# PEER routing in fewer DVE steps, one ring of gather buffers for u and v, and 768 gathered columns of v

## The chip, the cores and the metric

The kernel runs on one core of a Trainium2 chip. The metric is the device time of one execution in microseconds, the median of three runs. PE is the matrix engine, DVE the vector engine, ACT the scalar engine, POOL is GpSimd, SP the queue from which plain loads and stores are issued.

## The reference, cut to what matters

Two blocks follow each other on 256 tokens of width 2048, all in f32: a block of two layers (sparse attention, retention) and a block with an attention mixer and a PEER layer. The change lies in the PEER layer alone, which picks for each token and each of 8 heads 16 of 16,384 experts by two half keys of 128, and adds up the picked rows of v, weighted by the gelu of the product with the picked rows of u:

```python
def block(hb):                                   # 128 tokens at a time, D = 2048
    q = (hb @ w_query).reshape(PEER_BLOCK, PEER_HEADS, 2, D_KEY // 2)
    s = jnp.einsum('thpc,hpnc->thpn', q, sub_keys)
    top_s, top_i = lax.top_k(s, PEER_TOPK)
    cand_s = (top_s[:, :, 0, :, None] + top_s[:, :, 1, None, :]).reshape(PEER_BLOCK, PEER_HEADS, -1)
    cand_i = (top_i[:, :, 0, :, None] * N_KEYS + top_i[:, :, 1, None, :]).reshape(PEER_BLOCK, PEER_HEADS, -1)
    best_s, best_j = lax.top_k(cand_s, PEER_TOPK)
    idx = jnp.take_along_axis(cand_i, best_j, axis=-1)
    g = jax.nn.softmax(best_s, axis=-1)
    u_sel = jnp.take(u, idx, axis=0)
    a = jax.nn.gelu(jnp.einsum('thkd,td->thk', u_sel, hb), approximate=False)
    v_sel = jnp.take(v, idx, axis=0)
    return jnp.einsum('thk,thkd->td', (g * a), v_sel)
```

## The kernel before

The two attention blocks fill the first 1,780 us; their instructions are the same before and after the change. The PEER layer that follows is written as operations handed to a planner (`Plan`). Each has an engine, a cost in us, a key, what it waits for and which buffers of which ring it takes and frees. `run` keeps a clock for each engine, takes the operation that can start first (among near equals the one with the lowest key) and emits it; the order in which each engine then executes is fixed. Transfers are modelled by one rate, 340 KB per us, and operations marked `two` on DVE and POOL exclude each other in the plan.

The stages of the PEER layer, by what they compute:

- **Queries and routing** (`plan_query`, `plan_route`): 16 units, one for each head and half of the tokens (t). In a unit, DVE takes the best 16 of each half key's 128 scores (L2026, L2027), adds them to 256 candidate sums (`cand`, L1553), takes the best 16 of those with their places `bj` (a row and a column of the 16 x 16 sums, L1563 and L1564), casts the places to bf16 (L1566), marks the place of each among 16 (`eq`, L1568), multiplies the marks with the half keys' indices `tif` (cast at L1551, multiplied at L1579), and sums along the last axis to two numbers each (`keyno`, L1581). The expert's row number is formed from the two (`idx`, L1584 and L1585). POOL negates the largest sum (`nm`, L1573, an operation of its own in the plan), and ACT takes the exponential for the softmax (L1576).
- **Gathers of u** (`plan_gather_u`): for each of the 256 pairs (head, rank, t) one indirect DMA from POOL's queue (L1684) fetches 128 rows of the first 1,024 columns of u, 512 KB. Its product with the tokens is either one DVE instruction (a dot, L1690; 167 of them) or a product on POOL (L1696, 89) with a sum on ACT (L1697). The planner chooses.
- **Scores** (`plan_scores`): the other 1,024 columns of u are loaded in full, 128 blocks of 128 experts, 512 KB each. They are transposed on PE, split into a high part (`uhi`, ACT, L1738) and a rest (`ulo`, DVE, L1742), and multiplied with the tokens (L1750 to L1752) into the table `S` of 128 x 128 x 256.
- **Picks** (`plan_digits`, `plan_keyno`, `plan_pick`, `plan_coef`): 64 groups of four tokens. One-hot rows come out of a product of digit codes (the far product, L1800, and a Relu on ACT, L1804), multiply `S` on PE (L1809), and a select on DVE (`pjunk`, L1815) takes the picked scores. The codes come from a constant `spread` that is loaded when the stage opens and multiplied out on DVE (`digits`, L1434).
- **Weights** (`plan_weights`): the picked experts' weights are written back over `S`, again with one-hot products (`ohb`, L1877; S copied by ACT, L1892).
- **v** (`plan_gather_v`, `plan_out`): for the first GV = 736 columns of v, 256 indirect gathers (L1925) are each scaled and added into `vacc` by DVE (L1932). The first 90 (EARLY) start when their buffers allow, the others are paced by the dense loads. The other 1,312 columns are loaded in full, 128 tiles of 128 experts (`vraw`, L1959); ACT makes `vhi` (L1963) and `wh`, DVE `vlo` (L1967) and `wl` (L1975), and PE runs 18 matmuls on each (L1980): three products, two halves of the tokens, pieces of 512, 512 and 288 columns.

Buffers around it: three slots for gathers of u in the early pool `ud`, and three more (`rg`) once routing is over. The early ones are given up when the scores near their end; the last gathers of u, and four buffers (`rx`) for gathers of v, go on side by side, and when the last dot is done the three of `rg` join the ring of v. The slots of `vraw` (four) lie in a pool that also holds the picks' and the weights' one-hot tiles and is opened anew (`open_out`) when the weights are done.

## Time and profile before

| | us |
|---|---|
| median of 3 runs | 3259.75 |
| lowest, highest | 3255.08, 3261.12 |
| the profiled execution | 3261.98 |
| its span, first to last instruction | 3260.3 |

Over the span PE is busy 2897.5 us (89%), DVE 2422.6 (74%), ACT 1550.9 (48%) and POOL 1113.1 (34%); the mean granted TensorE clock is 0.950 of full speed. A busy matrix engine over the whole span doesn't mean that it bounds each stage: the slices of the page show its share, the clock and the DMA rate rise and fall with the stages, and a stage is read by the engine or the queue that has no idle time in it. Durations below come from the profiled execution.

### The profile page before, as it was taken

How to read it: one execution, taken by the hardware profiler on the slowest of the kernel's cores; microseconds unless marked ns; L12 is line 12 of the kernel's file. 1: busy time of each engine (PE TensorE's matmuls, PEld its weight loads, DVE VectorE, ACT ScalarE, POOL GpSimd, SP SyncE). 2: the span in 40 equal slices, each digit the busy share in tenths (PEclk: the TensorE clock that was granted, in tenths of full speed). 3: DMA queues.
4: the chain of work that ended last, by engine and by line, in shares of the span. 5: the costliest groups of instructions: out<-in, count | busy, mean ns of one | idle time of the engine just before them, and what ended most of it. 6: DMA issues, size and time to landing. Idle time of an engine off the chain costs nothing.

```text
span 3260.3 us, 46369 instructions
## 1 busy us (share of the span) xinstructions
PE 2897.5 (89%) x16646; PEld 2461.6 (76%) x16646; DVE 2422.6 (74%) x4207; ACT 1550.9 (48%) x2529; POOL 1113.1 (34%) x805
## 2 busy tenths in 40 slices
PE   3598989789999999999998769798887799799998
PEld 1386667667788779888887768788886587688887
DVE  7969886867856654565555989778786789788886
ACT  5555554545444544454554435434343258344443
POOL 3324431412000000000000445557776657555541
PEclk9699999899999999999998989999998699899999
DMA  8777886766555554545456536799996558999997
GB/s 297 243 242 246 279 273 186 249 211 215 174 165 164 162 175 128 164 125 148 130 181 223 172 117 217 258 348 332 326 329 220 187 171 253 339 343 333 334 332 231
DMA packets 294611, 751.52 MB, mean 231 GB/s; under 512 B 33518, under 2 KB 40612, under 8 KB 293996
## 3 DMA queue, kind: packets, MB, share of 16 engines
q1 hardware_dynamic: 236432, 515.65, 49.9%
q0 software_dynamic: 57344, 230.72, 20.3%
q8 instruction: 131, 2.15, 0.3%
q10 hardware_dynamic: 604, 2.19, 0.2%
q14 instruction: 100, 0.82, 0.1%
HBM read 741.64 MB, written 6.82 MB: 230 GB/s over the span
## 4 chain that ended last, share of the span: by engine, by line
PE 53%; DVE 15%; DMA 12%; issue 6%; POOL 6%; ACT 3%; SPq 0%; DVEq 0%; POOLq 0%; ACTq 0%
PE b_mm L1980 11%; PE b_mm L393 7%; PE b_mm L394 7%; PE b_mm L392 7%; DMA mraw<-in_w_mod 6%; DMA gathered<-in_peer_u,idx 5%; PE b_at L1980 3%; DVE gathered L1690 2%; PE b_mm L414 2%; PE b_mm L412 2%; POOL gathered L1684 2%; PE b_mm L413 2%; DVE lo L367 2%; POOL gathered L1696 2%; PE b_at L1809 2%
## 5 line engine op out<-in xcount | busy, mean ns | idle before, releaser
L367 DVE TENSOR_TENSOR lo<-raw,hi 128x1024 fp32r<-128x1024 f32 (+2 forms) x456 | 573.7, 1260 | 351.7 <-ACT hi L366 349.8
L366 ACT CAST hi<-raw 128x1024 fp32r<-128x1024 f32 (+2 forms) x456 | 464.4, 1021 | 454.1 <-PE b_mm L394 285.1
L393 PE MATMUL b_mm<-lo,hh 128*128 128x512 f32 (+1 forms) x1536 | 620.6, 405 | 39.0 <-DVE lo L367 35.9
L394 PE MATMUL b_mm<-hi,hl 128*128 128x512 f32 (+1 forms) x1536 | 604.7, 398 | 0.3 <-DVE hl L644 0.3
L392 PE MATMUL b_mm<-hi,hh 128*128 128x512 f32 (+1 forms) x1536 | 580.7, 401 | 9.6 <-ACT hi L366 6.6
L1925 POOL DMA_INDIRECT gathered<-in_peer_v,idx x256 | 324.8, 1269 | 251.8 <-DVE vacc L1932 226.6
L1684 POOL DMA_INDIRECT gathered<-in_peer_u,idx x256 | 295.8, 1155 | 286.7 <-ACT gathered L1697 163.9
L393 PEld LDWEIGHTS b_mm<-lo,hh 128*128 128x128 f32 x1536 | 295.7, 192 | 118.5 <-DVE lo L367 59.6
L392 PEld LDWEIGHTS b_mm<-hi,hh 128*128 128x128 f32 x1536 | 292.6, 191 | 84.0 <-ACT hi L366 11.2
L394 PEld LDWEIGHTS b_mm<-hi,hl 128*128 128x128 f32 x1536 | 294.1, 192 | 63.0 <-DVE hl L644 1.7
L560 POOL TENSOR_TENSOR macc<-macc,mraw 128x512 f32<-128x512 f32 x112 | 183.9, 1642 | 419.1 <-ACT mraw L558 386.9
L1752 PE MATMUL b_mm<-hd,ulo 128*128 128x256 f32 x1024 | 301.3, 294 | 28.9 <-DVE ulo L1742 28.7
L1750 PE MATMUL b_mm<-hd,uhi 128*128 128x256 f32 x1024 | 309.4, 302 | 12.5 <-ACT uhi L1738 11.7
L1690 DVE SCALAR_TENSOR_TENSOR gathered<-gathered,hn 128x1024 f32<-128x1024 f32 x167 | 255.9, 1551 | 77.7 <-DMA gathered<-in_peer_u,idx 76.7
L1751 PE MATMUL b_mm<-hd,uhi 128*128 128x256 f32 x1024 | 295.5, 289 | 0.0
L1932 DVE SCALAR_TENSOR_TENSOR vacc<-gathered,cf,vacc 128x736 f32<-128x736 f32 x256 | 250.7, 979 | 9.4 <-DMA gathered<-in_peer_v,idx 8.4
L1752 PEld LDWEIGHTS b_mm<-hd,ulo 128*128 128x128 f32 x1024 | 201.7, 197 | 39.6 <-DVE ulo L1742 39.1
L1967 DVE TENSOR_TENSOR vlo<-vraw,vhi 128x1312 fp32r<-128x1312 f32 x128 | 195.1, 1524 | 46.6 <-ACT vhi L1963 46.6
L1696 POOL TENSOR_TENSOR gathered<-gathered,hn 128x1024 f32<-128x1024 f32 x89 | 213.6, 2400 | 20.4 <-DMA gathered<-in_peer_u,idx 18.9
L1963 ACT CAST vhi<-vraw 128x1312 fp32r<-128x1312 f32 x128 | 165.7, 1294 | 107.3 <-PE b_at L1980 99.3
L1750 PEld LDWEIGHTS b_mm<-hd,uhi 128*128 128x128 f32 x1024 | 202.3, 198 | 16.7 <-ACT uhi L1738 16.7
L1751 PEld LDWEIGHTS b_mm<-hd,uhi 128*128 128x128 f32 x1024 | 202.4, 198 | 0.0
(615 smaller groups left out, 6036.8 us busy)
## 6 DMA issues: line engine op xcount, KB each, us to landing
raw<-in_w_in SPq DMA_DIRECT2D x336, 512.0 KB
mraw<-in_w_mod SPq DMA_DIRECT2D x192, 512.0 KB
vraw<-in_peer_v SPq DMA_DIRECT2D x128, 656.0 KB
uraw<-in_peer_u SPq DMA_DIRECT2D x123, 512.0 KB
raw<-in_w_out SPq DMA_DIRECT2D x96, 512.0 KB
raw<-in_peer_w_query SPq DMA_DIRECT2D x32, 512.0 KB
raw<-in_w_in SPq DMA_DIRECT2D x16, 256.0 KB
gathered<-in_peer_u,idx POOLq DMA_INDIRECT x256, 7.0
```

Source lines behind the costliest of these rows:

```text
L366: nc.scalar.copy(hi[:, :, :n], raw[:, :, :n])
L367: nc.vector.tensor_tensor(lo[:, :, :n], raw[:, :, :n], hi.bitcast(F32)[:, :, :n], ALU.subtract)
L392: nc.tensor.matmul(o, ah[:, kk, s], hi[:, k, :n], start=kk == 0, stop=False)
L393: nc.tensor.matmul(o, ah[:, kk, s], lo[:, k, :n], start=False, stop=False)
L394: nc.tensor.matmul(o, al[:, kk, s], hi[:, k, :n], start=False, stop=kk == KT - 1)
L1684: nc.gpsimd.indirect_dma_start(out=g, out_offset=None, in_=rows, in_offset=bass.IndirectOffsetOnAxis(ap=self.idx[h, t][:, k:k + 1], axis=0))
L1690: nc.vector.scalar_tensor_tensor(s["g"], s["g"], 1.0, self.hn[:, t, :], op0=ALU.mult, op1=ALU.mult, accum_out=a)
L1750: nc.tensor.matmul(o, h["hi"][:, k, :], hh[:, kk, :], start=kk == 0, stop=False)
L1751: nc.tensor.matmul(o, h["hi"][:, k, :], hl[:, kk, :], start=False, stop=False)
L1752: nc.tensor.matmul(o, h["lo"][:, k, :], hh[:, kk, :], start=False, stop=kk == UD - 1)
L1925: nc.gpsimd.indirect_dma_start(out=g, out_offset=None, in_=rows, in_offset=bass.IndirectOffsetOnAxis(ap=self.idx[h, t][:, k:k + 1], axis=0))
L1980: nc.tensor.matmul(acc[t, q][:, :w], s[a][:, t * P:(t + 1) * P], s[b][:, c - GV:c - GV + w], start=e == 0 and n == 0, stop=e == P - 1 and ...
```

## The change

- `GV` goes from 736 to 768: 1,280 dense columns in pieces of 512, 512 and 256; gathers of v are 384 KB instead of 368, dense tiles 640 KB instead of 656. The planner's rate is 330 instead of 340 KB per us.
- In a routing unit the half indices are cast by two ACT instructions that also scale them (the first half by 128 and the row pitch of 16, the second by 16), the places are cast by ACT, and one reduce over both halves of `eq` gives the row number at once, which ACT casts to an integer in `idx`, now one tile for each t. The two DVE instructions that combined the halves and the two DVE casts are gone. POOL's negation is issued along with the places and is no longer an operation of the plan.
- The digits and the number of a pick's group of experts (`key`) are taken from `idx` by shifts and masks; for the latter DVE gets a shift and a cast for each t, and one transpose of one tile stands where there was one of two.
- The early pool has four gather slots; `rg` has two, and the four of `rx` are added to the same ring when the picks open. The gathers of v use that ring too and come after the last gather of u.
- The slot for the first dense tile of v has a pool of its own, so that it is loaded when the picks open; the tiles after it wait for `open_out` as before.

```diff
-GV = 736
+GV = 768
...
+    RATE = 330.0
...
-                self.transfers = max(self.transfers, t) + kb / 340.0
+                self.transfers = max(self.transfers, t) + kb / self.RATE
...
-        self.gu = Ring([(self.ud, "g%d" % i) for i in range(3)], any=True)
-        self.gv = Ring([], any=True)
+        self.gu = Ring([(self.ud, "g%d" % i) for i in range(4)], any=True)
...
     def open_more(self, o):
         self.qs.close()
         self.rg = self.pool(self.st, "rg")
-        self.gu.add([(self.rg, "g%d" % i) for i in range(3)], self.plan.now)
+        self.rows[1] = self.rg.tile([P, 8 * P], BF16, name="rows1")
+        self.gu.add([(self.rg, "g%d" % i) for i in range(2)], self.plan.now)
...
     def open_pick(self, o):
...
-        self.gv.add([(self.rx, "x%d" % i) for i in range(RX)], self.plan.now)
+        self.gu.add([(self.rx, "x%d" % i) for i in range(RX)], self.plan.now)
+        self.vraw = self.pool(self.st, "vr")
...
+        def scaled(o):
+            s["indf"] = sp.tile([P, 2, TOPK], BF16, name="tif", tag="tif", bufs=2)
+            for p in range(2):
+                nc.scalar.activation(s["indf"][:, p, :], s["ind"][:, p, :], AF.Copy, scale=float((P, 1)[p] * (D // UNIT)))
+
         def sums(o):
             val = s["val"]
-            s["indf"] = sp.tile([P, 2, TOPK], BF16, name="tif", tag="tif", bufs=2)
-            nc.vector.tensor_copy(s["indf"], s["ind"])
...
         def places(o):
             bj = s["bj"]
+            nm = s["nm"] = sp.tile([P, 1], F32, name="nm", tag="nm", bufs=2)
...
-            bf = sp.tile([P, 2, TOPK], BF16, name="bf_", tag="bf_", bufs=2)
-            nc.vector.tensor_copy(bf, bj)
...
+            nc.gpsimd.tensor_scalar(nm, s["best"][:, 0:1], -1.0, None, op0=ALU.mult)
+
+        def exps(o):
+            s["bf"] = sp.tile([P, 2, TOPK], BF16, name="bf_", tag="bf_", bufs=2)
+            nc.scalar.copy(s["bf"], s["bj"])
+            nc.scalar.activation(self.gw[t][:, o_], s["best"], AF.Exp, bias=s["nm"], accum_out=self.sums[t][:, h:h + 1])
...
-            pick = self.keyno[t][:, :, o_]
-            nc.vector.tensor_reduce(pick, s["eq"], AX.X, ALU.add)
...
-            nc.vector.scalar_tensor_tensor(idx, pick[:, 0, :], float(P), pick[:, 1, :], op0=ALU.mult, op1=ALU.add)
-            nc.vector.tensor_scalar(idx, idx, D // UNIT, None, op0=ALU.mult)
...
+            nc.vector.tensor_reduce(s["n"], eq.rearrange("p a k j -> p k a j"), AX.XY, ALU.add)
+
+        def whole(o):
+            nc.scalar.copy(self.idx[t][:, o_], s["n"])
...
-        m = plan.op("POOL", 0.2, negated, b0 - 20, after=[z])
-        x = plan.op("ACT", 0.5, exps, b0, after=[m], signals=[self.summed[t]])
-        b = plan.op("DVE", 1.2, places, b0, after=[z], takes=[eq], two=True)
-        n = plan.op("DVE", 1.9, numbers, b0, after=[b], frees=[(eq, b)], two=True)
+        m = plan.op("DVE", 0.4, places, b0 - 10, after=[z], two=True)
+        x = plan.op("ACT", 0.75, exps, b0 - 10, after=[m], signals=[self.summed[t]])
+        n = plan.op("DVE", 1.85, numbers, b0, after=[x], two=True)
+        n = plan.op("ACT", 0.3, whole, b0 - 20, after=[n])
...
+        def first(o):
+            n = self.lp.tile([P, P], I32, name="key", tag="key")
+            s["f"] = self.lp.tile([P, P], F32, name="keyf", tag="keyf")
+            nc.vector.tensor_scalar(n, self.idx[t], 11, None, op0=ALU.logical_shift_right)
+            nc.vector.tensor_copy(s["f"], n)
+
         def turn(o):
-            s["ps"] = self.transpose4([self.keyno[t][:, p, :] for p in range(2)])
+            s["ps"] = self.transpose4([s["f"]])
...
-        n, last = 0, [chosen]
+        n, last = 0, [chosen, self.last_gather]
...
+    def raw_v(self, o):
+        n = o.held[self.ring("vraw", VRAW)][0][1]
+        return (self.vp if n else self.vraw).tile([P, D - GV], F32, name="vraw", tag="vraw%d" % n)
...
-            a = plan.op("SP", 0.1, load, key - 30, after=[opened] if e == 0 else [la], takes=[rr],
+            a = plan.op("SP", 0.1, load, key - 30, after=[chosen] if e == 0 else [la, opened] if e == 1 else [la], takes=[rr],
```

Three places where the planner's order differs. First DVE, in one routing unit, from the places of the best sums on; `x3` counts equal rows in a row. Before:

```order
L1563 TENSOR_SCALAR bj<-bj 128x16
L1564 TENSOR_SCALAR bj<-bj 128x16
L1566 CAST bf__16089<-bj 128x32
L1568 TENSOR_TENSOR eq<-bf__16089,iotab 128x512
L1579 TENSOR_TENSOR eq<-eq,tif 128x512
L1581 TENSOR_REDUCE keyno_14631<-eq 128x2x16
L1584 SCALAR_TENSOR_TENSOR idx<-keyno_14631 128x16
L1585 TENSOR_SCALAR idx<-idx 128x16
L1742 TENSOR_TENSOR ulo<-b_tr,uhi 128x512 x3
L1551 CAST tif<-ti 128x32
L1553 TENSOR_TENSOR cand<-tv 128x256
```

After:

```order
L1562 TENSOR_SCALAR bj<-bj 128x16
L1563 TENSOR_SCALAR bj<-bj 128x16
L1742 TENSOR_TENSOR ulo<-b_tr,uhi 128x512 x3
L1573 TENSOR_TENSOR eq<-bf__16288,iotab 128x512
L1575 TENSOR_TENSOR eq<-eq,tif 128x512
L1577 TENSOR_REDUCE num<-eq 128x16
L1551 TENSOR_TENSOR cand<-tv 128x256
```

Four rows are gone, and three `ulo` stand between the places and the comparison. When the last unit's number is formed, DVE has done 14 dots and 72 `ulo`, where it had done 8 and 77; POOL has issued 47 gathers of u and done 31 products, where it had 43 and 35.

Second DVE again, from the end of the scores to the first selects of the picks. Before:

```order
L1742 TENSOR_TENSOR ulo<-b_at,uhi 128x512
L1690 SCALAR_TENSOR_TENSOR gathered,act_14636<-gathered,hn 128x1024 x2
L1434 TENSOR_TENSOR digits<-spread 128x1024
L1690 SCALAR_TENSOR_TENSOR gathered,act_14636<-gathered,hn 128x1024 x2
L1815 SCALAR_TENSOR_TENSOR pjunk,dots_22904<-iota_22908,byexp_22906,b_at 128x128 x16
L1690 SCALAR_TENSOR_TENSOR gathered,act_14636<-gathered,hn 128x1024 x2
```

After:

```order
L1689 SCALAR_TENSOR_TENSOR gathered,act_14635<-gathered,hn 128x1024
L1435 TENSOR_TENSOR digits<-spread 128x1024
L1689 SCALAR_TENSOR_TENSOR gathered,act_14635<-gathered,hn 128x1024 x3
L1784 TENSOR_SCALAR key<-idx_14629 128x128
L1785 CAST keyf<-key 128x128
L1689 SCALAR_TENSOR_TENSOR gathered,act_14635<-gathered,hn 128x1024
L1784 TENSOR_SCALAR key<-idx_14630 128x128
L1785 CAST keyf<-key 128x128
L1689 SCALAR_TENSOR_TENSOR gathered,act_14635<-gathered,hn 128x1024 x2
L1822 SCALAR_TENSOR_TENSOR pjunk,dots_22912<-iota_22916,byexp_22914,b_at 128x128 x8
L1689 SCALAR_TENSOR_TENSOR gathered,act_14635<-gathered,hn 128x1024 x9
L1822 SCALAR_TENSOR_TENSOR pjunk,dots_22912<-iota_22916,byexp_22914,b_at 128x128 x8
```

On PE the first far product now stands behind the transpose of `keyf`. Nine dots stand in a row after eight selects, where selects and pairs of dots alternated; four gathers of v went ahead of the last gather of u before, and none do now.

Third DVE from the last `ohb` of the weights to the first `vlo` of dense v. Before:

```order
L1877 SCALAR_TENSOR_TENSOR ohb<-b_mm,byexp_22907 128x512
L1932 SCALAR_TENSOR_TENSOR vacc<-gathered,cf_23638,vacc 128x736 x6
L1975 TENSOR_TENSOR wl<-S,wh 128x256 x2
L1932 SCALAR_TENSOR_TENSOR vacc<-gathered,cf_23638,vacc 128x736 x5
L1967 TENSOR_TENSOR vlo<-vraw,vhi 128x1312 x2
```

After:

```order
L1884 SCALAR_TENSOR_TENSOR ohb<-b_mm,byexp_22915 128x512
L1938 SCALAR_TENSOR_TENSOR vacc<-gathered,cf_23695,vacc 128x768 x5
L1985 TENSOR_TENSOR wl<-S,wh 128x256
L1938 SCALAR_TENSOR_TENSOR vacc<-gathered,cf_23695,vacc 128x768
L1977 TENSOR_TENSOR vlo<-vraw,vhi 128x1280
L1985 TENSOR_TENSOR wl<-S,wh 128x256
L1977 TENSOR_TENSOR vlo<-vraw,vhi 128x1280
```

Six adds of v stand ahead of the first `vlo` instead of eleven.

## Rows read from the trace of the kernel before

**Rows 1.** Windows of the span by stage: busy us of each engine, clock, DMA.
```profile
core 0: us, PE busy (x) PEld busy (x) DVE busy (x) ACT busy (x) POOL busy (x), PEclk, DMA share, GB/s
1781.70:2068.20 286.50, 230.72 (x1849) 225.44 (x1848) 261.07 (x660) 128.35 (x251) 138.79 (x97) 0.93 0.55 177
...
2150.00:2300.00 150.00, 135.67 (x1093) 129.44 (x1093) 122.06 (x165) 58.81 (x111) 107.61 (x77) 1.00 0.94 340
2300.00:2482.00 182.00, 161.96 (x1280) 154.66 (x1279) 143.56 (x186) 75.02 (x143) 134.81 (x92) 0.98 0.87 314
2482.00:2495.60 13.60, 0.31 (x3) 0.07 (x1) 1.27 (x2) 1.05 (x3) 7.40 (x8) 0.65 0.87 295
2495.60:2600.00 104.40, 83.59 (x328) 63.51 (x329) 72.41 (x328) 33.40 (x58) 62.63 (x45) 0.71 0.56 179
...
2771.00:2797.20 26.20, 8.99 (x25) 7.11 (x26) 14.29 (x17) 5.67 (x7) 13.74 (x13) 0.54 0.96 353
...
2850.00:3200.00 350.00, 350.00 (x1768) 299.98 (x1767) 301.38 (x332) 167.16 (x197) 182.13 (x136) 1.00 0.95 335
```

**Rows 2.** Groups by line and form, DVE, 1780 to 2110 us.
```profile
L1584 DVE SCALAR_TENSOR_TENSOR idx<-keyno 128x16 int32<-128x16 f32 x16 | 22.6, 1413 | 0.6
...
L1585 DVE TENSOR_SCALAR idx<-idx 128x16 int32<-128x16 int32 x16 | 5.6, 348 | 0.6
...
L1551 DVE CAST tif<-ti 128x32 bf16<-128x32 uint32 x16 | 2.9, 180 | 0.0
...
L1566 DVE CAST bf__15773<-bj 128x32 bf16<-128x32 uint32 x1 | 3.0, 2957 | 0.0
...
L1690 DVE SCALAR_TENSOR_TENSOR gathered<-gathered,hn 128x1024 f32<-128x1024 f32 x16 | 20.0, 1270 | 7.3 <-DMA gathered<-in_peer_u,idx 7.3
...
L1742 DVE TENSOR_TENSOR ulo<-b_tr,uhi 128x512 fp32r<-128x512 f32 x63 | 42.5, 683 | 12.4 <-ACT uhi L1738 12.1
...
L1563 DVE TENSOR_SCALAR bj<-bj 128x16 uint32<-128x16 uint32 x16 | 11.0, 688 | 0.1
```

**Rows 3.** Timeline of DVE and of POOL: start, duration, engine, line, operation.
```profile
1946.87 2.99 DVE L1584 SCALAR_TENSOR_TENSOR idx<-keyno 128x16 int32<-128x16 f32 x1
...
1947.42 2.40 POOL L1696 TENSOR_TENSOR gathered<-gathered,hn 128x1024 f32<-128x1024 f32 x1
...
2002.04 0.18 DVE L1584 SCALAR_TENSOR_TENSOR idx<-keyno 128x16 int32<-128x16 f32 x1
```

**Rows 4.** Groups by line and form, ACT, 1780 to 2110 us.
```profile
L1576 ACT ACTIVATE gw<-best,nm 128x16 f32<-128x16 f32 x16 | 4.9, 307 | 7.4 <-DVE best L2026 4.8 <-POOL nm L1573 2.6
```

**Rows 5.** Chain of waits; groups of PE and DVE, 2495 to 2771 us.
```profile
2482.60 11.60 DMA spread<-const_spread
...
L1809 PE MATMUL b_at<-S,ohf 128*128 128x128 f32 x512 | 124.1, 404 | 18.7 <-DVE pjunk L1815 18.7
...
L1690 DVE SCALAR_TENSOR_TENSOR gathered<-gathered,hn 128x1024 f32<-128x1024 f32 x36 | 43.8, 1224 | 23.4 <-DMA gathered<-in_peer_u,idx 22.8
```

**Rows 6.** Timelines of PE, ACT and DVE at the start of dense v.
```profile
2780.03 1.22 PE L1980 MATMUL b_mm<-vhi,wh 128*128 128x512 f32 x2 [9.41 <-ACT vhi L1963]
...
2778.69 1.28 ACT L1963 CAST vhi<-vraw 128x1312 fp32r<-128x1312 f32 x1 [6.25 <-DMA vraw<-in_peer_v]
...
2778.08 0.98 DVE L1932 SCALAR_TENSOR_TENSOR vacc<-gathered,cf,vacc 128x736 f32<-128x736 f32 x1 [3.56 <-DMA gathered<-in_peer_v,idx]
...
2795.30 1.05 PE L1980 MATMUL b_mm<-vhi,wh 128*128 128x512 f32 x2
```

**Rows 7.** Timeline of PE: neighbours in dense v and in the scores.
```profile
2806.54 0.29 PE L1980 MATMUL b_at<-vhi,wl 128*128 128x288 f32 x1
...
2806.68 0.63 PE L1980 MATMUL b_mm<-vhi,wh 128*128 128x512 f32 x2
...
2470.08 0.28 PE L1750 MATMUL b_mm<-hd,uhi 128*128 128x256 f32 x1
...
2470.20 0.28 PE L1751 MATMUL b_mm<-hd,uhi 128*128 128x256 f32 x1
```

More of the change, by code (lines that the diff above doesn't have):

```diff
@@ L1343, in peer_start @@
         nc.gpsimd.tensor_copy(self.iota, iota)
-        self.rows = [None, up.tile([P, 8 * P], BF16, name="rows1")]
-        self.keyno = [up.tile([P, 2, P], F32, name="keyno%d" % t) for t in range(2)]
+        self.idx = [self.rp.tile([P, P], I32, name="idx%d" % t) for t in range(2)]
+        self.rows = [None, None]
         self.sums = [up.tile([P, PH], F32, name="sums%d" % t) for t in range(2)]
@@ L1383, in peer @@
             plan.op("SP", 0.4, back, 600, after=[chosen], kb=128, signals=[self.rowed[p]])
-        keyno = [self.plan_keyno(t, chosen) for t in range(2)]
+        keyno = [self.plan_keyno(0, chosen)]
+        keyno.append(self.plan_keyno(1, keyno[0]))
         self.cf_done = []
@@ L1388, in peer @@
             self.cf_done.append(self.plan_coef(t))
-        dotted = plan.op("ctl", 0, self.open_ring, 0, after=self.dotted)
         for t in range(2):
@@ L1392, in peer @@
         self.plan_gather_v(units, chosen)
-        out = plan.op("ctl", 0, self.open_out, 0, after=[self.weighed, dotted])
-        self.plan_out(out)
+        out = plan.op("ctl", 0, self.open_out, 0, after=[self.weighed, *self.dotted])
+        self.plan_out(out, chosen)
         plan.run()
@@ L1427, in open_pick @@
         self.dots = [self.lp.tile([P, P], F32, name="dots%d" % t) for t in range(2)]
-        self.byexp = [self.lp.tile([P, 3, P], F32, name="byexp%d" % t) for t in range(2)]
+        self.byexp = [self.lp.tile([P, 2, P], F32, name="byexp%d" % t) for t in range(2)]
         self.iota = self.numbers(self.lp, P)
@@ L1436, in open_pick @@
             ALU.mult), 0, after=[o], signals=[self.far])
-    def open_ring(self, o):
-        for s in self.gu.slots:
-            assert s[0] is not None
-        self.gv.add([s[1] for s in self.gu.slots], self.plan.now)
-        self.gu.slots = []
     def open_out(self, o):
@@ L1701, in plan_gather_u @@
                 last = [o.issued]
+                self.last_gather = o.issued
                 plan.choice([("DVE", 1.31, dot, (), 0, True), ("POOL", 2.45, product, (poolq,), 0, True)], key,
@@ L1779, in plan_keyno @@
         s = {}
+        def first(o):
[3 more added lines that the diff above has]
+            nc.vector.tensor_copy(s["f"], n)
         def turn(o):
-            s["ps"] = self.transpose4([self.keyno[t][:, p, :] for p in range(2)])
+            s["ps"] = self.transpose4([s["f"]])
         def move(o):
-            nc.scalar.copy(self.byexp[t][:, 0:2, :], s["ps"][:, :2 * P].rearrange("p (a n) -> p a n", a=2))
-        a = plan.op("PE", 0.4, turn, 590, after=[chosen], takes=[ring("tr", 2)])
-        return plan.op("ACT", 0.5, move, 590, after=[a], frees=[(ring("tr", 2), a)])
+            nc.scalar.copy(self.byexp[t][:, 0, :], s["ps"][:, :P])
+        a = plan.op("DVE", 0.45, first, 590, after=[chosen], two=True)
+        a = plan.op("PE", 0.2, turn, 590, after=[a], takes=[ring("tr", 2)])
+        return plan.op("ACT", 0.4, move, 590, after=[a], frees=[(ring("tr", 2), a)])
     def plan_pick(self, t, after):
@@ L1957, in load @@
             def load(o, e=e, s=s):
-                s["raw"] = self.vp.tile([P, wide], F32, name="vraw", tag="vraw", bufs=VRAW)
+                s["raw"] = self.raw_v(o)
                 nc.sync.dma_start(s["raw"], v[e])
@@ L2004, in load @@
                 def load(o, t=t, c=c, w=w, y=y):
-                    y["y"] = self.vp.tile([P, wide], F32, name="y", tag="vraw", bufs=VRAW)[:, :w]
+                    y["y"] = self.raw_v(o)[:, :w]
                     nc.sync.dma_start(y["y"], self.x_kept[:, t, c:c + w])
```

44 lines of the change are left out of this document (21 added, 23 removed).

## The prediction

> **What bounds the kernel now.** I read the busy time of each engine stretch by stretch first, since the change touches only the last 1,480 us (routing, expert scores, picks, weights, dense v), and the share of busy time over the whole span says nothing of a single stage. In [rows 1] the reader is to see five stages with five limits. From 1781.7 to 2068.2 us, while the 16 routing units run, VectorE is busy 261.07 of 286.50 us and the DMA engines only 0.55: DVE sets the pace. From 2150 to 2482 the DMA share is 0.94 and then 0.87 at 340 and 314 GB/s: the dense u loads and the u gathers set it. From 2482 to 2495.6 nothing runs but transfers (PE busy 0.31 us). In the next 104.4 us PE is busy 83.59, so idle 20.8, at a granted clock of 0.71. From 2771.0 to 2797.2 the switch from weights to dense v leaves PE at 8.99 of 26.20 us. From 2850 to 3200 PE is busy all 350.00 us at clock 1.00 (the 2.4 GHz level), with DMA at 0.95 and 335 GB/s close behind it. Then I went into each stage with the view that shows its limit: groups by line for DVE and ACT, the chain of waits at the two gaps, the sequence of instructions at the start of dense v.
>
> **Routing (DVE-bound).** Four kinds of instruction leave DVE, 16 of each: the combination of the two numbers L1584 (22.6 us), its scaling L1585 (5.6), the cast of the half indices L1551 (2.9), and the cast of the places L1566, of L1551's shape and time except for one at 2,957 ns (15 x 0.18 + 2.957 = 5.7) [rows 2]. That is 36.8 us of busy time. Not all of it is work: the same L1584 takes 2.99 us where a product on POOL starts beside it and 0.18 us alone [rows 3]; 16 x (1.413 - 0.18) = 19.8 us of that row is waiting, and of L1585 (16 x 0.17) and the one L1566 likewise 2.7 and 2.8, 25.2 together. Sure are 36.8 - 25.2 = 11.6 us. The other 25.2 either vanish or move to the next DVE instruction that meets the product. By the printed order DVE also does 14 instead of 8 dots before the last routing operation (6 x 1.270 = 7.6 us more) and 72 instead of 77 ulo of its half (5 x 0.683 = 3.4 us less) [rows 2]. So DVE gains between 11.6 - 7.6 + 3.4 = 7.4 and 32.6 us. The nearest row for either end is L1563, which stays and already stands at 688 ns for 16 columns [rows 2]: some waiting does land on whatever comes. I take the middle, 20.
>
> Against it stand new costs on ACT. Four small operations per unit at up to 0.307 us are 16 x 1.2 = 20 us of an engine that is busy 128.35 of 286.50 [rows 1, 4]; the three ulo that the order now puts between the places and the comparison cover the cast. But the exponential waits for nm, which POOL computes behind whatever product it has begun, 2.40 us each [rows 3], and ACT, in order, holds the next uhi behind it; DVE already lost 12.1 us waiting for uhi [rows 2]. Before, with nm placed on POOL by the planner, this wait was 2.6 us in all [rows 4]; now nm is issued wherever POOL's program happens to stand. Bounds: 0 and 16 x 2.4 = 38. I take 8, a fifth of the upper end, as ACT is idle more than half the time. Routing: -20 + 8 = **-12** (from -32.6 to +31.0).
>
> **Scores and gathers, 2068 to 2482.** Same bytes: 2.5 dense tiles more are left, 4 gathers fewer, each 512 KB, so 1.5 x 512 KB less transferred before. The fourth early buffer feeds a stage that DMA already fills. **0**, bounds -14 (182 us at 314 GB/s brought to 340: 182 x (1 - 314/340)) [rows 1] and +8 (at its end two late buffers instead of three, one gather each four dots late: 36 dots waited 22.8 us for gathers with three [rows 5], a third of that).
>
> **Picks and weights.** The 13.6 us gap is a constant's transfer of 11.60 us in the chain [rows 5]; it stays, since the digits it feeds still wait for it. Behind it the first far product now stands behind a transpose that waits for a shift and a cast on DVE, which stand behind three more dots: 3 x 1.22 [rows 5] + about 0.5 (two 128-column steps, nearest rows 0.18 and 0.69 us for 16 and 512 columns [rows 2, 3]) = 4.2, say 4.4 with the transpose. What is queued behind it is all of PE. Against that, the last u gathers have six buffers instead of three, and no early v gather before them: the 22.8 us that DVE waited for gathers [rows 5] nearly go, and with them much of the 18.7 us that PE's picks waited for the selects [rows 5]. But nine dots in a row (11 us) now stop the selects once, while PE has work for two groups, so about 8 of that returns. 4.4 + 8 - 15.5 = **-3**; bounds -16 (nothing returns: 4.4 - 20.8) and +10 (only a sixth of the idle goes).
>
> **Switch to dense v.** PE waited 9.41 us for vhi; vhi itself had waited 6.25 us for the load, which could not be issued before the weights' pool closed, and vlo stood behind 11 adds of v, one of which waited 3.56 us for its gather; the second tile started at 2795.30 [rows 6]. With a buffer of its own the first tile is there long before. vhi can run at 2773.4, when the last weights are copied, 5.3 us earlier; vlo stands behind six adds instead of eleven (5 x 0.98, and some waits less). The first tile then ends at 2783 to 2785. The second tile's load is issued when the first was before and lands around 2778.7, the landing that vhi showed, so it isn't in the way. **-11**, bounds -6 (only the add's part, 5 x 0.98 and one wait) and -15.
>
> **Dense v.** 128 tiles x 6 last pieces = 768 matmuls go from 288 to 256 columns. In 350 us 1,768 matmuls ran, 98.2 tiles of 18, 3.563 us each [rows 1]; by columns (7,872 a tile) 0.453 ns each, 768 x 32 x 0.453 = 11.1 us. Rows put 0.14 us between a 288-column one and the next, and 0.12 between two of 256 columns [rows 7]: 15 us, with two-digit rounding; with 0.130 by columns against 0.12 it is 7.9. I take **-10.5**. What hides behind PE: DMA needs 1.194 MB a tile (335 x 3.563); gathers grow by 21.6 KB a tile (1.35 of them at 16 KB more), the load shrinks by 16, so 1.200 MB in 3.48 us, 345 GB/s. The stage ran at 335 with a share of 0.95, and 353 stands in the rows once, at 0.96 [rows 1]. It just fits. One v buffer fewer (six for seven) costs nothing while gathers are paced by the loads. An add of 768 columns for 736 costs DVE 0.04 us, 6 us in all, on an engine busy 301 of 350.
>
> **Sum.** -12 + 0 - 3 - 11 - 10.5 = -36.5. Against the profiled execution's own 3261.98 us that is 3225.5; this execution lies 2.2 us above the median of the runs, which I carry over: **3223 us**.
>
> **Rivals.** *B, the waits vanish.* If what stalls DVE is specific to the removed kinds, routing gains all 32.6 and ACT costs nothing: 3259.75 - 32.6 - 24.5 = 3203. For it: ulo, which reads one operand from PSUM, stands at 683 ns over 63 of them [rows 2], as if it met no product. Against it: L1563 at 688 ns, and the products don't get fewer by much (35 to 31). The Trainium skill, "SBUF — State Buffer", section "Who interferes with whom", says that a DVE instruction with two SBUF inputs or in a two-port mode and a GpSimd one lock each other out for a whole instruction, while a reduce never does; by it the ulo and maxima behind the reduce don't inherit its stalls, which gives this rival's time. The 2.99 us beside the 2.40 us product agree with the lock; no row shows the rest.
>
> *C, DMA becomes the bound of dense v.* If 335 GB/s is what the queues give, a tile takes 1.200 / 0.335 = 3.58 us, 0.02 more than now, and the gain of 10.5 becomes a loss of 128 x 0.02 = 2.5: 3259.75 - 12 - 3 - 11 + 2.5 = 3236. For it: 0.95 share in [rows 1]. Against: 353 GB/s.
>
> *D, ACT behind POOL: slower.* The exponential waits out a product in all 16 units, +38.4, with the DVE gain at 7.4: routing +31.0, the rest -24.5, so +6.5, 3266. It decides from 2.0 us exposed per unit ((24.5 + 7.4) / 16). For it: nm is not in the plan. Against: half of POOL's time is gathers and waits (138.79 of 286.50 busy), and ACT's slack.
>
> *E, the early load does nothing it says.* If the second tile, not the first, sets the end of the switch (three loads issued at once at 353 GB/s, 0.96 busy), the 11 us go: 3234.
>
> **How the numbers follow.** My forecast, A, 0.55; B 0.15; C 0.17; D 0.07; E 0.06. About 0.2% (6.5 us) is what a measurement of this kernel can tell from no change, so all but D end below 3253: faster 0.90, with 0.03 taken off for terms that miss together; slower 0.06, D nearly whole; same 0.04. The range reaches from B with a third of the gather stage's lower bound, 3198, to C with half of the picks' way to their upper end, 3242; D lies outside, with the far tails of A.
>
> **What would show it.** In the trace after: routing ending some 12 us earlier, its DVE without L1584's row, and L1563 or the multiply of eq longer if the waits moved. ACT's exponential with large waits for nm would be D. The gap before the picks unchanged at about 13 to 18 us. The first dense tile done within 14 us of the last weight copy instead of 25. A stretch of 350 us of dense v with more than 1,800 matmuls and no PE wait for vhi; PE waits on vraw there would be C. I am wrong if the routing stage's length doesn't follow DVE, or if the gathers' buffers cost more than the picks give back.

## The result

The changed kernel takes 3219.85 us, median of four runs (3215.89 to 3241.63), against 3260.43 us before: the medians lie 40.6 us or 1.2% apart, and the ratio of the runs is 0.9888 (95% interval 0.9863 to 0.9913). 3223 was forecast. The profiled execution takes 3215.89 us, 46.1 less than that of before; the sum had said 36.5.

The time by stages, read from the same events in both traces (last reduce of routing, last product of the scores, last copy of the weights, start of the second dense tile, last dense product):

| stage | before | after | change | forecast |
|---|---|---|---|---|
| to the end of routing | 2067.8 | 2036.4 | -31.4 | -12 |
| scores | 414.1 | 400.1 | -14.0 | 0 |
| gap, picks and weights | 289.8 | 303.1 | +13.3 | -3 |
| switch to dense v | 23.6 | 15.7 | -7.9 | -11 |
| dense v | 453.8 | 447.5 | -6.3 | -10.5 |

So the total came out close while only the last two terms were near. The windows of the changed kernel by stage (busy us and instructions of each engine, granted clock, DMA share, GB/s), which answer to [rows 1]:

```profile
1781.50:2036.60 255.10, 218.44 (x1756) 214.54 (x1756) 230.68 (x606) 128.16 (x301) 138.15 (x99) 0.93 0.62 202
2036.60:2120.00 83.40, 79.96 (x665) 79.34 (x665) 62.00 (x111) 42.45 (x82) 60.27 (x43) 0.98 0.96 336
2120.00:2270.00 150.00, 134.34 (x1064) 128.73 (x1064) 116.70 (x161) 61.34 (x113) 113.04 (x77) 0.98 0.92 335
2270.00:2436.50 166.50, 152.05 (x1218) 145.55 (x1216) 122.78 (x172) 72.23 (x134) 124.02 (x86) 0.99 0.87 320
2436.50:2452.80 16.30, 0.39 (x2) 0.20 (x3) 5.57 (x10) 0.58 (x1) 6.89 (x8) 0.56 0.90 301
2452.80:2560.00 107.20, 74.91 (x293) 57.13 (x293) 95.42 (x315) 32.41 (x60) 84.92 (x59) 0.66 0.67 223
2739.60:2755.00 15.40, 6.65 (x17) 5.16 (x18) 7.55 (x8) 3.44 (x5) 7.90 (x7) 0.50 0.97 336
...
2810.00:3160.00 350.00, 350.00 (x1791) 297.33 (x1790) 303.78 (x334) 166.10 (x199) 161.84 (x135) 1.00 0.95 338
```

The first 83 us after routing run at 336 GB/s. The same stretch of before has no row in [rows 1]; it reads:

```profile
2068.00:2150.00 82.00, 64.34 (x483) 63.26 (x484) 53.77 (x105) 28.48 (x55) 41.55 (x34) 0.88 0.81 276
```

In routing and just behind it (1780 to 2080 us), DVE's groups by line and form (busy us, mean ns | idle before, releaser) and ACT's, which answer to [rows 2] and [rows 4]:

```profile
L1689 DVE SCALAR_TENSOR_TENSOR gathered<-gathered,hn 128x1024 f32<-128x1024 f32 x23 | 33.0, 1438 | 1.9 <-DMA gathered<-in_peer_u,idx 1.8
...
L1577 DVE TENSOR_REDUCE num<-eq 128x16 f32<-128x512 bf16 x16 | 11.0, 686 | 0.6
...
L1562 DVE TENSOR_SCALAR bj<-bj 128x16 uint32<-128x16 uint32 x16 | 4.9, 309 | 0.0
```
```profile
L1569 ACT ACTIVATE gw<-best,nm 128x16 f32<-128x16 f32 x16 | 4.9, 306 | 1.0 <-POOL nm L1564 1.0
```

The places' shift, 688 ns before, has fallen to 309: what waited on the removed instructions did not move there. The dots took some of it (1,438 ns for 1,270), and so did the comparison that makes `eq` (in the mean of 16, 843 ns for 692). The exponential waits for nm only 1.0 us in all 16 units together. Where a product runs on POOL, DVE now does maxima beside it at their usual 0.41 us (timelines of POOL and DVE):

```profile
1934.13 2.41 POOL L1695 TENSOR_TENSOR gathered<-gathered,hn 128x1024 f32<-128x1024 f32 x1
```
```profile
1934.35 0.41 DVE L2036 MAX8 best<-cand 128x8 f32<-128x256 f32 x1
```

In the scores (2037 to 2437 us) the dots take 1.59 us in the mean, and POOL's group of gathers shows what the buffers were waited for; behind the second bar stands the time that the engine was idle before them:

```profile
L1689 DVE SCALAR_TENSOR_TENSOR gathered<-gathered,hn 128x1024 f32<-128x1024 f32 x117 | 182.8, 1586 | 24.3 <-DMA gathered<-in_peer_u,idx 24.1
```
```profile
L1683 POOL DMA_INDIRECT gathered<-in_peer_u,idx x160 | 188.8, 1180 | 101.3 <-DVE gathered L1689 40.8 <-ACT gathered L1696 24.4 <-issue 23.0
```

In the picks, DVE's last dots are half again as long as in [rows 5], and PE waits for them in one piece (groups of DVE from 2436.5 to 2739.6; then PE's waits, as engine, line, what ended them, us in total, times, longest):

```profile
L1689 DVE SCALAR_TENSOR_TENSOR gathered<-gathered,hn 128x1024 f32<-128x1024 f32 x36 | 66.2, 1872 | 3.8 <-DMA gathered<-in_peer_u,idx 3.6 <-DMA vraw<-in_peer_v 0.2
```
```profile
PE b_at L1816 <- DVE pjunk L1822: 21.2, 6, 13.0
...
PE b_tr L422 <- DVE keyf L1785: 15.9, 1, 15.9
```

The 22.8 us that dots waited for gathers have become 3.6, but each dot takes 1.87 us for 1.22 next to the products on POOL: 36 x 0.65 = 23 us. At the switch, vhi follows the last copy at once. PE stands 2.7 us for it instead of 9.4 [rows 6], and 7.1 for vlo, which comes behind adds that wait for their gathers (timelines of PE, then DVE):

```profile
2741.25 1.22 PE L1990 MATMUL b_mm<-vhi,wh 128*128 128x512 f32 x2 [2.72 <-ACT vhi L1973]
...
2750.85 1.22 PE L1990 MATMUL b_mm<-vlo,wh 128*128 128x512 f32 x2 [7.10 <-DVE vlo L1977]
```
```profile
2745.42 1.02 DVE L1938 SCALAR_TENSOR_TENSOR vacc<-gathered,cf,vacc 128x768 f32<-128x768 f32 x1 [2.91 <-DMA gathered<-in_peer_v,idx]
...
2748.37 1.02 DVE L1938 SCALAR_TENSOR_TENSOR vacc<-gathered,cf,vacc 128x768 f32<-128x768 f32 x1 [1.60 <-DMA gathered<-in_peer_v,idx]
```

Before, PE stood for vlo about as long (PE's waits from 2771 to 2797 us of that trace):

```profile
PE b_mm L1980 <- DVE vlo L1967: 8.2, 1, 8.2
```

### The profile page after: what moved, and what is told of

It is laid out like the page before. It is cut to its first block, busy times and chain, and to the rows that moved or that the text cites. A ratio compares the mean times of both kernels' runs of the same rounds, so it can differ in the third digit from the quotient of the medians.

```text
span 3214.2 us, 46345 instructions
## 1 busy us (share of the span) xinstructions
PE 2884.2 (90%) x16644; PEld 2446.5 (76%) x16644; DVE 2397.3 (75%) x4143; ACT 1557.9 (48%) x2593; POOL 1105.9 (34%) x805
## 4 chain that ended last, share of the span: by engine, by line
PE 59%; DVE 13%; DMA 10%; POOL 5%; issue 5%; ACT 3%; ACTq 0%; POOLq 0%; DVEq 0%; SPq 0%
PE b_mm L1990 11%; PE b_mm L394 7%; PE b_mm L393 7%; DMA mraw<-in_w_mod 7%; PE b_mm L395 7%; PE b_at L1816 3%; PE b_at L1990 3%; DVE gathered L1689 3%; PE b_mm L415 2%; POOL gathered L1683 2%; PE b_mm L413 2%; PE b_mm L414 2%; PE b_tr L422 2%; PE b_mm L1752 2%; DVE lo L368 2%
## 5 line engine op out<-in xcount | busy, mean ns | idle before, releaser
L1931 POOL DMA_INDIRECT gathered<-in_peer_v,idx x256 | 309.6, 1209 | 311.8 <-DVE vacc L1938 278.0
L1750 PE MATMUL b_mm<-hd,uhi 128*128 128x256 f32 x1024 | 308.6, 301 | 12.6 <-ACT uhi L1738 12.6
L1689 DVE SCALAR_TENSOR_TENSOR gathered<-gathered,hn 128x1024 f32<-128x1024 f32 x167 | 269.2, 1636 | 28.2 <-DMA gathered<-in_peer_u,idx 27.7
L1938 DVE SCALAR_TENSOR_TENSOR vacc<-gathered,cf,vacc 128x768 f32<-128x768 f32 x256 | 259.3, 1013 | 7.7 <-DMA gathered<-in_peer_v,idx 6.6
L1977 DVE TENSOR_TENSOR vlo<-vraw,vhi 128x1280 fp32r<-128x1280 f32 x128 | 190.7, 1490 | 58.9 <-ACT vhi L1973 58.9
L1973 ACT CAST vhi<-vraw 128x1280 fp32r<-128x1280 f32 x128 | 162.0, 1265 | 97.4 <-PE b_at L1990 97.4
```

Of the source, the lines that this page charges most:

```text
L1689: nc.vector.scalar_tensor_tensor(s["g"], s["g"], 1.0, self.hn[:, t, :], op0=ALU.mult, op1=ALU.mult, accum_out=a)
L1750: nc.tensor.matmul(o, h["hi"][:, k, :], hh[:, kk, :], start=kk == 0, stop=False)
L1931: nc.gpsimd.indirect_dma_start(out=g, out_offset=None, in_=rows, in_offset=bass.IndirectOffsetOnAxis(ap=self.idx[t][:, h * TOPK + k:h * TO ...
```

## The experiments

Each edit is to the changed kernel unless said otherwise. Runs of one group share a chip. On the chip of the first group the clock granted in the weights stage fell to 0.50 while PE was busy, and that stage is some 37 us longer in all four profiles there. So those runs are read by stage up to the first weights (the first one-hot row `ohb` of the weights) and by the ratio to before on that chip (3294.68 us).

**Routing undone.**

```diff
-            nc.vector.tensor_reduce(s["n"], eq.rearrange("p a k j -> p k a j"), AX.XY, ALU.add)
-            nc.scalar.copy(self.idx[t][:, o_], s["n"])
+            nc.vector.tensor_reduce(pick, s["eq"], AX.X, ALU.add)
+            nc.vector.scalar_tensor_tensor(idx, pick[:, 0, :], float(P), pick[:, 1, :], op0=ALU.mult, op1=ALU.add)
+            nc.vector.tensor_scalar(idx, idx, D // UNIT, None, op0=ALU.mult)
...
```

> The changed kernel with the routing unit of before put back (two DVE casts, the reduce to two numbers, the two DVE instructions that form the row number, POOL's negation as an operation of the plan); buffers, columns and the rest as changed. Theory 1 (the routing stage lost 31.6 us because DVE's waits behind POOL products sat on the removed instructions and did not move to what follows): routing lasts 283 to 288 us again instead of 255.0, with the combining instruction near 1.4 us each, and the kernel is 27 to 33 us slower than the changed one. Rival 1 (only the work went, the waits would have moved on; the rest of the 31.6 came from the fourth early buffer and from the order): routing 266 to 270 us, kernel 11 to 15 us slower. For the scores stage: if its 13.8 us came from the fourth early buffer, it stays at 400 us here; if it came from the routing's casts, it is back at 414.

Routing is back at 291.6 us, longer than either theory had it, with the combining instruction at 1,290 ns and the shift of the places at 774. But the ratio is 0.9881 (0.9850 to 0.9911): no slower than the changed kernel's 0.9888. From the end of routing to the first weights it took 511 us for 538, and the planner, with another order before it, chose 22 products on POOL after routing instead of 56. The stage was right, the total was not, and a second thing had moved; the runs without late products below show that it was the reason.

**A probe on the lock.** One two-operand instruction of 16 columns behind the reduce, without effect:

```diff
+            nc.vector.scalar_tensor_tensor(s["n"], s["n"], 1.0, s["n"], op0=ALU.mult, op1=ALU.max)
```

> The changed kernel with one more DVE instruction in each routing unit: right behind the reduce, a two-operand instruction of 16 columns on the row numbers that leaves them as they are (16 in all; it does no work). Theory 1 (an instruction with two SBUF operands that is next after the reduce takes the wait for the POOL product; the reduce and the maxima that follow do not): it lasts about 1.2 to 1.4 us in the mean, up to 3 us beside a product, as the combining instruction did; routing 15 to 22 us longer than the changed kernel's 255.0. Rival 1 (the wait hung on that one instruction's form, from f32 to an integer, or on something else that went with it): about 0.18 us each, routing 3 us longer.

Routing: 271.6 us, 16.7 longer. Its DVE groups in routing: the probe, and the mask of the places, which grew from 186 ns:

```profile
L1578 DVE SCALAR_TENSOR_TENSOR num<-num 128x16 f32<-128x16 f32 x16 | 13.7, 856 | 0.6
...
L1563 DVE TENSOR_SCALAR bj<-bj 128x16 uint32<-128x16 uint32 x16 | 8.5, 529 | 0.5
```

856 ns is less than expected, yet nearly five times the 180 ns that the combining instruction took alone [rows 3]. So the wait did not hang on the removed instruction itself: another one behind the reduce takes it. The mask, which has one operand, and the comparison (1,220 ns for 843) grew too. The maxima keep their time. So does the reduce, at 686 ns, but in these traces a product begins at most 0.36 us before its end, so that no reduce ran beside one from its start.

**Three early buffers, and rings apart.**

```diff
-        self.gu = Ring([(self.ud, "g%d" % i) for i in range(4)], any=True)
+        self.gu = Ring([(self.ud, "g%d" % i) for i in range(3)], any=True)
```

> The changed kernel with three early gather buffers instead of four. Theory 2 (the fourth buffer is what lifts the transfers in the first 80 us after routing from 276 to 336 GB/s, and so made the scores stage 13.8 us shorter): scores stage 410 to 414 us instead of 399.8, its first 80 us below 300 GB/s, DVE waiting some 50 us for gathers instead of 24; kernel 8 to 14 us slower than the changed one. Rival 2 (the transfers rose because digits and casts left DVE and POOL there): 400 us, 336 GB/s, kernel within 3 us of the changed one plus what the picks lose by a few more bunched dots.

```diff
-        self.gu.add([(self.rx, "x%d" % i) for i in range(RX)], self.plan.now)
+        self.gu.add([(self.rx, "x0")], self.plan.now)
+        self.gv.add([(self.rx, "x%d" % i) for i in range(1, RX)], self.plan.now)
...
```

> The changed kernel with two rings again in the picks: three buffers for the last gathers of u (two of rg, one of rx) and three for v until the last dot, as three and four before. DVE's order in the picks then is 2 or 3 dots between 8 or 12 selects again, not nine in a row. Theory 3 (the picks and weights became 10.7 us longer because six buffers let the last dots come in a block of nine, each held up by a product on POOL, while PE stands): no PE wait of 12.95 us in the picks, first far product to last weight copy 274 to 280 us instead of 286.8, kernel 6 to 12 us faster than the changed one. Rival 3 (the picks are longer because the dots met more POOL products or a lower clock, whatever their order): 285 us or more, kernel within 3 us.

With three early buffers both theory 2 and rival 2 miss. The first 80 us did fall, to 306 GB/s, but the scores stage shrank to 372 us: fewer gathers had been done in it (64 were left instead of 46), and the picks paid it back, 158 us to the first weights. This run doesn't isolate the buffer, for the planner's choice moved with it: 33 products on POOL in the scores instead of 44, and dots of 1.28 us there instead of 1.59. With the rings apart the products are the same in number. PE's longest wait in the picks fell from 13.0 to 4.6 us, as theory 3 has it, and the dots back to 1.24 us, yet the scores took 404.9 and the picks began no sooner. From the end of routing to the first weights the four kernels need 538.6 (before), 537.9 (after), 536.0 and 538.8 us. So the -14 of the scores and the +13 of the picks are one thing, counted on two sides of a border: the gathers must be through before the weights, and buffers only shift where they run. The ratios, 0.9871 and 0.9853, have intervals that reach to 0.990 and 0.988, and that of the changed kernel, on another chip, reaches down to 0.9863. So theory 3's total, some 11 us by the ratio of the run with the rings apart, is neither shown nor excluded.

**The changed kernel again, the first tile's load later in the order, 736 columns, no late products**, on one chip:

> The changed kernel once more, beside the next ones on their chip, since the chips differ (in the runs so far on another chip, the granted clock fell to 0.50 in the weights stage, in every kernel). Every theory expects 0.987 to 0.990 of the time of before on the same chip, routing 255, scores 400, picks up to the first weights 121 us.

3222.17 us, 0.9886 (0.9862 to 0.9910); scores 400.2, picks to the first weights 122.1, and 8.2 us from the last weight copy to the end of the second vlo, where the same kernel took 12.9 in the first profile. That much this switch differs between two executions of one kernel.

```diff
-            a = plan.op("SP", 0.1, load, key - 30, after=[chosen] if e == 0 else [la, opened] if e == 1 else [la], takes=[rr],
+            a = plan.op("SP", 0.1, load, key - 30, after=[opened] if e == 0 else [la], takes=[rr],
```

> The changed kernel with the first dense tile of v loaded when the weights' pool closes, as before, instead of in a buffer of its own. Theory 4 (the early load is what made the switch from the last weight copy to the second vlo 7.5 us shorter): switch 6 to 9 us longer than in the changed kernel beside it, and so is the kernel. Rival 4 (the switch is set by the adds of v ahead of vlo, which wait for their gathers; the early load doesn't matter): switch within 2 us, kernel within 3.

The switch takes 5.2 us and the kernel 3214.02 (0.9854, 0.9823 to 0.9886). But this run doesn't test the load. The edit moves it in the planner's order alone; its buffer is still one of its own, and the transfer is issued as early as in the changed kernel, some 290 us ahead of the switch (timeline of SP, in this run and in the changed kernel):

```profile
2452.27 0.44 SPq L1969 DMA_DIRECT2D vraw<-in_peer_v  x1
```
```profile
2447.83 0.44 SPq L1969 DMA_DIRECT2D vraw<-in_peer_v  x1
```

So theory 4 is not refuted by it. What does differ is DVE: two adds fewer stand between the last `ohb` and vlo, and the four that do run without a wait (timeline of DVE in this run):

```profile
2742.41 4.18 DVE L1938 SCALAR_TENSOR_TENSOR vacc<-gathered,cf,vacc 128x768 f32<-128x768 f32 x4
```

That is 3.0 us less than beside it, within what two executions of the changed kernel differ. What the early load is worth comes out of a later pair of runs on one chip, the kernel before and the changed buffers, both without late products.

> The changed kernel with 736 gathered columns of v again, so 288 columns in the last piece. Theory 5 (a matmul of 288 columns takes 8.4 ns longer than one of 256, 132.6 against 124.2 ns between neighbours in the two traces): dense v from the second vlo to the last matmul 6 to 7 us longer, kernel 5 to 8 us slower. Rival 5a (time goes by columns, and the changed kernel loses part of it to gathers): 10 to 11 us. Rival 5b (transfers bound the stage and more gathered bytes cost what fewer columns give): within 2 us.

With `GV = 736` dense v takes 454.0 us from the start of the second tile to the last product, where the changed kernel beside it takes 447.4; neighbours stand 132.6 and 124.2 ns apart in the mean in the traces of before and after [rows 7]. Theory 5 has the stage. (From the second vlo, as the expectation counts, it is only 2.4 us, as this vlo came late, behind adds.) The total, 3217.49 us (0.9868, 0.9844 to 0.9891), doesn't show it: 6 us are about what the runs spread.

```diff
-                plan.choice([("DVE", 1.31, dot, (), 0, True), ("POOL", 2.45, product, (poolq,), 0, True)], key,
+                plan.choice([("DVE", 1.31, dot, (), 0, True), ("POOL", 2.45, product, (poolq,), 0, True)][:1 if n >= 50 else 2], key,
```

> The changed kernel in which no gather of u from the 51st on may be a product on POOL: all later dots are DVE's (routing keeps its products). Theory 6 (from the end of routing to the first weights, the transfers are held back not by the DMA engines but by gather buffers that wait for a product on POOL and its sum on ACT, and by dots that the products lock out, 1.6 us instead of 1.23; with routing undone, where the planner chose 10 products instead of 44 there, the transfers ran at 375 GB/s instead of 335): from the end of routing to the first weights 505 to 520 us instead of 538, kernel 18 to 32 us faster than the changed one. Rival 6 (DVE, with 56 dots of 1.23 us more, becomes the bound, or the 335 GB/s are all there is): 532 us or more, kernel within 6 us or slower.

3174.68 us, 0.9737 (0.9715 to 0.9759): 47 us faster than the changed kernel beside it, more than theory 6 asked, with 497 us from the end of routing to the first weights. The window of its scores stage and DVE's group of dots there:

```profile
2036.00:2397.00 361.00, 350.87 (x2954) 346.94 (x2953) 320.93 (x553) 131.78 (x245) 198.95 (x172) 1.00 0.99 383
```
```profile
L1689 DVE SCALAR_TENSOR_TENSOR gathered<-gathered,hn 128x1024 f32<-128x1024 f32 x171 | 206.2, 1220 | 15.6 <-DMA gathered<-in_peer_u,idx 15.4
```

DVE does 55 more dots, 54 of them here, and the stage is 39 us shorter: dots at 1.22 us, transfers at 383 GB/s where 335 had looked like their limit.

**What each part is worth with that out of the way**, on a third chip:

> The routing unit of before put back, and no products on POOL from the 51st gather on, so that the number of products is the same as in the run without late products. It tells what the routing part is worth when the planner's choice of products doesn't change with it. Theory 1 (routing is bound by DVE and its gain is carried to the end, but for what the transfers do meanwhile: 8 ulo more, 2 gathers fewer, about 3 us): routing 286 to 292 us, kernel 28 to 36 us slower than the run without late products. Rival 1b (the transfers catch up, since they bound the next stage; the routing part was worth little, as undoing it alone suggested): 15 us or less.

The routing edit and the edit on products stand together. The kernel takes 3208.26 us (0.9834, 0.9802 to 0.9866); by the ratios, as the chips differ, that is some 32 us slower than without late products alone. Routing takes 293.2 us, 39 more than there. With the number of products held (37 and 34), theory 1 has the total: most of what the routing part saves in its stage reaches the end, and the stages up to the first weights win 8 us back.

The edit on products alone, on the kernel before:

> The kernel before with one edit: no products on POOL from the 51st gather on. Theory 6 (products hold the transfers back, in the kernel before as well): its scores stage at 370 GB/s or more, from the end of routing to the first weights 500 to 520 us instead of 538.6, kernel 20 to 36 us faster than before, 0.989 to 0.994. Rival 6b (it takes the changed buffers, four early ones and one ring, to use the freed transfers): 530 us or more, kernel within 8 us of before.

3215.29 us, 0.9866 (0.9843 to 0.9889): 43 us, more than expected and as much as the whole change. From the end of routing to the first weights 501.6 us, and the window of its scores stage reads

```profile
2066.60:2437.50 370.90, 346.50 (x2850) 340.82 (x2851) 323.44 (x560) 124.97 (x232) 203.65 (x178) 0.97 0.97 374
```

Within their intervals the two add up: 0.9888 and 0.9866 apart, 0.9737 together.

These last two runs also tell what the early load does. In the kernel before without late products no add stands between the last weight copy and vlo, and vlo waits for vhi, and vhi for its tile (timelines of ACT and DVE; then PE's waits in the switch, in this run and in the one with the routing unit of before, which has the early load):

```profile
2736.00 1.28 ACT L1963 CAST vhi<-vraw 128x1312 fp32r<-128x1312 f32 x1 [5.71 <-DMA vraw<-in_peer_v]
```
```profile
2737.32 1.53 DVE L1967 TENSOR_TENSOR vlo<-vraw,vhi 128x1312 fp32r<-128x1312 f32 x1 [6.54 <-ACT vhi L1963]
```
```profile
PE b_mm L1980 <- ACT vhi L1963: 8.8, 1, 8.8
```
```profile
PE b_mm L1986 <- ACT vhi L1969: 2.7, 1, 2.7
```

The second tile starts 13.9 us after the last copy in the first of the two, and 7.0 us after it in the second. Where no add holds vlo up, then, the early load is worth about 7 us. The two runs also differ in routing, columns and buffers; the waits in the switch show none of these, but they were not taken out one by one.

```diff
...
+                            *([self.begun] if n >= 87 else [])
...
```

> The changed kernel in which the adds of v from the 88th on wait until the first vlo of dense v is made. Theory 4b (the switch is set by the last adds ahead of vlo, which wait for gathers that compete with the dense loads; with the tile loaded late two adds fewer stood there and the switch took 5.2 us instead of 8.2 to 12.9): switch from the last weight copy to the second vlo 4.5 to 6.5 us, PE waits for the first vlo under 2 us, kernel 2 to 7 us faster than the changed one. Rival 4c (it isn't the adds: PE's low clock and the second tile's load set it): 8 us or more, kernel within 2 us.

(`begun` is signalled by the first vlo.) PE's wait for the first vlo is gone, the switch takes 6.9 us to the end of the second vlo, and the kernel 3218.61 (0.9889, 0.9840 to 0.9938), no better. From the first far product to the last weight copy it takes 291.5 us, where two executions of the changed kernel took 286.8 and 288.2; whether holding the adds back costs that is open.

> The version that the runs point to: the changed kernel with no products on POOL from the 51st gather on, the last dots' keys spread over the picks of the first half of the tokens, and the first vlo ahead of the adds. Against the run without late products alone (0.9737 of before), whose gap before the picks is 17.1 us because the shift and cast of the expert numbers stand behind dots, and whose switch is 5.0 already: gap 13 to 14 us, switch the same, kernel 2 to 6 us faster, 0.972 of before. Rival: the spread dots hold up the weights of the first half; no gain or 3 us slower.

```diff
+                            key if n < 208 else 600.0 + 1.45 * (n - 208),
```

3153.76 us, 0.9674 (0.9652 to 0.9695), with this line beside the two edits above: 104.6 us faster than before, and by the ratios some 70 faster than the changed kernel and 20 faster than without late products alone, where 2 to 6 were expected. The gap is 13.0 us instead of 17.2, the weights begin 111 us after it instead of 118, and they take 8 us less, at a granted clock of 0.98 instead of 0.93. The spread keys and the earlier vlo stand in one run, so their shares are not separated, and the clock's part isn't known to come from either. Its windows of the gap and of the picks to the first weights:

```profile
2396.90:2409.90 13.00, 0.41 (x2) 0.23 (x3) 2.15 (x4) 0.57 (x1) 4.25 (x6) 0.68 0.94 315
2409.90:2520.90 111.00, 96.01 (x369) 71.72 (x369) 87.80 (x390) 26.97 (x48) 50.04 (x38) 0.64 0.56 176
```

## Why the prediction was right, and where it was not

The time, the sign and the range held; three of five terms did not. Of their errors (-19, -14, +16, +3 and +4 us) the second and third are one thing on two sides of a border, as the runs with other buffers show. The others leave -10 in the profiled executions and 3 us in the medians, and that they cancel so far is luck.

- **Routing, -12 against -31.4.** The mechanism was right, the size was off in both of its halves. Of DVE's gain, 7.4 to 32.6 were bounded and the middle, 20, taken; it was close to the upper end. The row that decided for the middle, the shift of the places at 688 ns, was itself a victim of the old order: it fell to 309, and stands at 774 with the routing unit of before put back. Rival B had this term. The Trainium skill's rule in "SBUF — State Buffer", "Who interferes with whom", that a DVE instruction with at most one SBUF input, outside the two-port modes, does not contend with GpSimd, and one with two such inputs does, fits the maxima at 0.41 us beside a product and the probe at 856 ns. Whether the shift and the mask, which wait too and have one operand, ran in a two-port mode, no run here shows. The 8 us for ACT behind POOL were nothing: 1.0 us of waits. Rival D had no ground.
- **Scores, 0 against -14.0.** The step that failed is that DMA "already fills" this stage. Its first 82 us, at 276 GB/s, were left out of the reading, and for the rest a share of 0.87 to 0.94 was taken for a limit. It was the products on POOL that held the transfers below it; without them the same transfers run at 0.99. The working also left out what its own counts say, that 1.5 x 512 KB less remained to be moved, an estimate of 2 us at the 335 GB/s of the rows.
- **Gap, picks and weights, -3 against +13.3,** above the bound of +10 (its own working, with a sixth of 20.8 us gone, gives 8.9). The gap's +2.6 was in the working (4.4). The block of nine dots was seen and priced at 8; what was missing is that the dots, no longer waiting for gathers, would meet the products, 1.87 us each. But by the runs with other buffers this term and the one before must be read together, and then they are -0.7 against -3.
- **Switch, -11 against -7.9.** The size was near (a second execution of the changed kernel has -12.6), with the last copy put at 2773.4 where it ended at 2771.7. That the early load takes away PE's wait for vhi held: 9.4 us became 2.7. But in both kernels the last wait of the switch is for vlo behind the adds. It began 17.5 us after the last copy before and 9.7 after, while vhi, with the late load, was done 8.3 us after it. So by these rows the adds that ended sooner gave most of this pair's gain; no run separates the two here. The load's turn comes where no add holds vlo up: without late products the early one is worth about 7 us. Rival E's reason does not show: in both traces PE goes from the first tile to the second without a wait.
- **Dense v, -10.5 against -6.3.** Time goes neither by columns nor by the rounded rows. A matmul of 256 columns follows 8.4 ns sooner than one of 288, 768 x 8.4 = 6.5 us, and the run with 736 columns gives 6.6. Rival C's limit was not met: 338 GB/s at an unchanged share of 0.95.

Not separated is how much of a late product's cost is the lock on DVE's dots (117 in the scores x 0.37 = 43 us of DVE time) and how much the gather buffer held through POOL and ACT; no run changed one without the other. That products kept POOL from issuing gathers is a third way that no run takes out. Against it speaks that POOL stood idle 101.3 us before its gathers in the scores, 40.8 until a dot and 24.4 until ACT's sum gave a buffer back.

## What to carry to other kernels

A transfer share of 0.9 isn't proof that transfers bound a stage: ask what holds the buffers, and take that away once. Moving work to an idle engine can cost more than it saves when the two engines lock each other; count what the helped engine's other instructions take beside it. When a planner chooses between engines, compare variants only after counting its choices, since undoing one part can move another. And look in the trace whether an edit did what it was meant to do: here a load that was moved back in the planner's order was issued as early as before.

## What the runs showed of the hardware

DVE maxima keep their time beside a POOL product of 2.41 us. A two-operand instruction of 16 columns that takes 180 ns alone took 2.99 us beside one, and 856 to 1,413 ns in the mean of the 16 in these runs; the shift of the places, with one operand, took 688 in the mean before; and a dot took 1.6 to 1.9 us in the stages with products for 1.22 without. Indirect gathers and plain loads together sustain 383 GB/s at a share of 0.99 over 361 us. And the granted clock was 0.50, the lower of its two levels, for some 80 to 90 us in which PE was fully busy, in all four profiles on one chip (below a window of the weights stage in the run with the rings apart, columns as above). On another chip it was 0.59 in the last 25 us of that stage in the run without late products, with PE busy 23.95:

```profile
2700.00:2750.00 50.00, 50.00 (x272) 42.84 (x272) 31.16 (x39) 27.16 (x34) 24.50 (x21) 0.50 0.58 165
```
